# Layer 0 of a two-layer decoder trunk: where the low parts of the weights and the second group's scans stand in the order of work

## The chip, the core and the metric

The kernel runs on one core of one Trainium2 chip. The core has five engines that run side by side and meet at semaphores: TensorE (PE, matrix products into PSUM, with its weight loads shown as PEld), VectorE (DVE), ScalarE (ACT), GpSimd (POOL) and SyncE (SP, which here issues most of the DMAs). DVE and ACT work through their instructions in the order in which the program gives them. The metric is the device time of one execution in microseconds, and the median of several executions is compared.

## The reference

The program computes a decoder trunk of two layers for 256 tokens of width 2048, in float32. Layer 0 is RMSNorm, one input projection to 6144 columns, two mixers side by side, an output projection, a residual and a squared-ReLU MLP. Layer 1 has dilated attention in place of the mixers and the same MLP. Only the mixers of layer 0 matter here:

```python
proj = h @ w_in
x_lru, y_lru, q_h, f_h, v_h, g_h = jnp.split(proj, list(IN_SPLITS), axis=-1)
lru = rg_lru(causal_depthwise_conv(x_lru, conv_w, conv_b), w_a, b_a, w_i, b_i, lam)
lru = lru * jax.nn.gelu(y_lru.astype(F32), approximate=True)
hg = hgrn2(q_h, f_h, v_h, g_h, lower_bound, g_norm)
mixed = jnp.concatenate([lru, hg], axis=-1).astype(h.dtype)
return mixed @ w_out
```

`rg_lru` makes two gates with small block matrices, turns them into `a` and `u` (a tanh, an exp and a square root for each), and runs the recurrence h = a h + u over the 256 tokens; the GeLU of `y` multiplies the result. `hgrn2` is a gated linear attention with eight heads: it multiplies running products of its forget gate into queries and keys, forms scores, mixes the values, normalises each head and multiplies with SiLU of `g`.

## The kernel before

**Products in three parts.** Every float32 weight tile is split into a high part (a cast to fp32r on ACT, the tile `hi`) and the low rest (a subtraction on DVE, the tile `lo`, which reads the raw weights and `hi`). Activations are split in the same way. A product is then three matmuls: high by high, high by low, low by high. They sum into a PSUM tile `p`.

**Units.** The weights come in units of 128 x 2048 floats, 1 MB each. The input projection has twelve groups of 512 columns, four units each, in the order of the string `ORDER`: `v0 x0 x1 q0 G0 f0 q1 f1 G1 v1 g0 y0 g1 y1` (`G0` and `G1` are the two units of gate weights). A unit of the projection is 24 matmuls with 512 columns. In the trace they can be counted; the groups begin at about 123.7 us (`q1`), 182 (`v1`), 209.5 (`g0`), 237.2 (`y0`), 262.9 (`g1`), 289.8 (`y1`) and 314 (the first pass of the output projection, `o0`); its second pass (`o1`) begins at about 338. When a unit begins, `unit` calls `fetch` for the unit two places later: its DMA, its cast on ACT and its low part on DVE. There are three buffers each for raw, high and low.

**Side work in lanes.** The mixers' own work is cut into steps, written as Python generators that stand in five lanes. Lanes `a` and `b` hold the hgrn chains, two heads each (`hgrn(0)` and `hgrn(1)`, then `hgrn(2)` and `hgrn(3)`, the second group). One step of a chain has a few small matmuls on PE, then several DVE instructions, then copies on ACT (`kc`) which the next step's matmuls read. Lane `c` holds the convolution, then the GeLU (`lru_gelu`, two steps for each half) and its products with the recurrence (`lru_out`). Lane `d` holds the normalisation and gating of the heads (`finish`). Lane `e` holds `lru_scan`, four steps for each half of the recurrence: two steps with tanh and exp, then two with the square root and the scans.

**The order by hand.** `TICKS` says which steps are issued where: for each group of columns eight entries, two for each unit, one after the unit's 12th matmul and one after its 24th. The letters of an entry name the lanes that move on one step. From the group `x0` on, `InOrder` chains all DVE instructions in program order, and all ACT instructions likewise; `mm` and `turn` chain the instructions of PE. So an instruction's place in the program is its place in its engine's queue. This ends with the last unit of `o0`; after it the order of DVE and ACT is left to the framework's scheduler.

**The low parts.** While entries of `TICKS` remain, `split` does not issue the low part at once; it puts it in the list `lows`, and `settle` issues what waits there. `settle` is called at the start of each unit and after each entry. So the low part of the unit two places on is issued in the middle of a unit, behind all steps of the entry there. The lines that matter are these:

```python
if at_ % 4 == 3 and ticks:
    tick(ticks.pop(0))
    settle()
```

In the profile, DVE and ACT instructions stand at line 68 (the wrapper that issues them), matmuls at 255 and transposes through PE at 258. So the instructions are told apart by their tiles: `lo<-raw,hi` is a low part, `hi<-raw` a high part, `xall`, `st` and `kc` belong to the hgrn chains, `xc` and `bufb` with 128x256 to the scans, `tk<-p` copies a finished group of columns out of PSUM, `hs`, `rs`, `hr`, `z` and `ho` belong to `finish`, and `tk<-tk` to the GeLU.

Of the kernel before, what the change touches and what calls it, by code (L numbers as in the profile page):

```python
# [41 lines left out]
def trunk_kernel(ctx, tc, head, x, xtok, xback, cols, tab, masks, pos, fin, w_in, w_gate, w_out, w_qkv, w_o, w1, w2, out):  # L42
# [195 lines left out]
    def settle():  # L238
        with stream():
            while lows:  # L240
                lows.pop(0)()

    def unit(src, i):
        settle()
        u = at[1]
        assert units[u][0] is src and units[u][1] in (None, i), (u, i)
        at[1] += 1
        if u + 2 >= at[0]:
            fetch()
        return made.pop(u)  # L250
# [3 lines left out]
    def mm(*args, **kw):  # L254
        chain[:] = [after(T.matmul(*args, **kw), chain)]  # L255
# [12 lines left out]
    def turn_some(age=2):  # L268
        for t in turns:
            t[0] += 1  # L270
        for _ in range(2):
            if turns and turns[0][0] >= age:
                turns.pop(0)[1]()
# [88 lines left out]
    def tokens(src, i0, mov, kgs=(0, 1, 2, 3), by_k=False, behind=(), then=()):  # L362
        ks = PAIRED if src is w_o else range(KB)
        ps = [pmm.tile([P, 512], F32, name="p") for _ in range(2)]
        for g in kgs:
            w = unit(src, i0 + g)
            order = [(j, i) for i in range(4) for j in range(2)] if by_k else \
                [(j, i) for j in range(2) for i in range(4)]
            for at_, (j, i) in enumerate(order):
                k = ks[4 * g + i]  # L370
                h, l = w.part(i * 512, 512)
                xh = mov[:, k, j * P:j * P + P]
                xl = mov[:, k, S + j * P:S + j * P + P]
                first, last = g == kgs[0] and i == 0, g == kgs[-1] and i == 3
                if g == kgs[-1] and (i, j) == (1, 0):
                    chain.extend(behind)
                mm(ps[j], xh, h, start=first, stop=False)
                mm(ps[j], xh, l, start=False, stop=False)
                mm(ps[j], xl, h, start=False, stop=last)
                if at_ % 4 == 3 and ticks:  # L380
                    tick(ticks.pop(0))
                    settle()
            turn_some(1)
            for f in steps.pop(0) if steps else ():
                f()
            for m in then[kgs.index(g)] if then else ():
                mixed_forms(m)
        return ps

    def tick(which):  # L390
        for name in which.strip("."):
            with urgent():
                while lanes[name] and next(lanes[name][0], True):
                    lanes[name].pop(0)

    def tokens_group(step, rt=None, by_k=False, behind=()):
        ticks[:] = TICKS.get(step, "").split()
        ps = tokens(w_in, 4 * PLACE[step], bufa, by_k=by_k)
        v = vgs.tile([P, 2, 512], F32, name="tk", bufs=7)
        with urgent():  # L400
            for j in range(2):
                after(A.activation(v[:, j], ps[j], AF.Copy, scale=1.0 if rt is None else rt[:, j:j + 1]), behind)
        return v
# [224 lines left out]
    def lru_in(n, half):  # L628
        b0 = 4 * n + 2 * half
        p = turned("po", [done[f"x{n}"]] * 2, (2 * half, 2 * half + 1), back=True)  # L630
        for i in range(2):
            b = b0 + i
            A.activation(xc[:, b], p[:, i], AF.Identity, bias=col("conv_b", b), scale=col("conv_w", 24 + b))
            for t in range(3):
                V.scalar_tensor_tensor(xc[:, b, 3 - t:], p[:, i, :S - 3 + t], col("conv_w", 8 * t + b),
                                       xc[:, b, 3 - t:], op0=OP.mult, op1=OP.add)
            yield
        split_to(bufb[:, b0:b0 + 2], xc[:, b0:b0 + 2])
        yield
# [14 lines left out]
    def lru_scan(gp):  # L654
        gr, gi = rooms[gp][:, :4], rooms[gp][:, 4:]
        for half in range(2):
            for m in range(2 * half, 2 * half + 2):
                b = 4 * gp + m
                V.tensor_tensor(xc[:, b], xc[:, b], gi[:, m], OP.mult)
                lut(gi[:, m], gr[:, m], AF.Tanh, scale=sp4[:, b:b + 1])  # L660
                lut(gr[:, m], gr[:, m], AF.Exp, scale=sp8[:, b:b + 1])
                V.tensor_scalar(gi[:, m], gi[:, m], -1.0, 1e-30, op0=OP.mult, op1=OP.max)
            yield
        for half in range(2):
            for m in range(2 * half, 2 * half + 2):
                b = 4 * gp + m
                lut(gi[:, m], gi[:, m], AF.Sqrt)
                V.scalar_tensor_tensor(gi[:, m], gr[:, m], 1.0, gi[:, m], op0=OP.add, op1=OP.mult)
                V.tensor_tensor(xc[:, b], xc[:, b], gi[:, m], OP.mult)
                V.tensor_tensor_scan(xc[:, b], gr[:, m], xc[:, b], 0.0, op0=OP.mult, op1=OP.add)  # L670
            yield

    def lru_gelu(n):
        y = done[f"y{n}"]
        q = outs[f"y{n}"] = vgs.tile([P, 2, 512], F32, name="tk", bufs=7)
        for j in range(2):
            A.activation(q[:, j], y[:, j], AF.Square, scale=math.sqrt(0.044715))
            V.scalar_tensor_tensor(q[:, j], q[:, j], 1.0, y[:, j], op0=OP.add, op1=OP.mult)
            lut(q[:, j], q[:, j], AF.Sigmoid, scale=2.0 * math.sqrt(2.0 / math.pi))
            V.tensor_tensor(y[:, j], y[:, j], q[:, j], OP.mult)  # L680
            yield

    def lru_out(n, half):
        b0 = 4 * n + 2 * half
        p = turned("pt" if half else "pd", [done[f"y{n}"]] * 2, (2 * half, 2 * half + 1), back=True)
        z = outs[f"y{n}"][:, half].rearrange("p (i s) -> p i s", i=2)
        V.tensor_tensor(z, p, xc[:, b0:b0 + 2], OP.mult)
        split_to(bufb[:, b0:b0 + 2], z)
        yield

    def reload():
        for j in range(2):
# [3 lines left out]
                 c=[lru_in(0, 0), lru_in(0, 1), lru_in(1, 0), lru_in(1, 1),  # L696
                    lru_gelu(0), lru_out(0, 0), lru_out(0, 1), lru_gelu(1), lru_out(1, 0), lru_out(1, 1)],
                 e=[lru_scan(0), lru_scan(1)],
# [17 lines left out]
    def close_mixers():  # L716
# [4 lines left out]
        pair, formh = open_pairs(0)  # L721

    tick("c")
    ticks[:] = TICKS["o0"].split()
    steps[:] = [[], [], [close_mixers], [lambda: setattr(InOrder, "on", False)]]
# [42 lines left out]
    def mixed_forms(m):  # L768
        z = pair.tile([P, 2, 2, P], F32, name="y1", bufs=2)
        b = bufb[:, 2 * m:2 * m + 2].bitcast(F32)  # L770
        V.tensor_tensor(z.rearrange("p i j c -> p i (j c)"), b[..., :S], b[..., S:], OP.add)
        a11, a21, a12, a22 = (z[:, i, j] for i in range(2) for j in range(2))
        combos(a22, a11, a21, a12, a11, a21, a12, a22)
        part_forms(formh, m, 1, slice(0, 4), z.rearrange("p i j (one c) -> p one (i j) c", one=1))

    def out_project(src, gname, kgs, behind=()):
        nrm = Norm()
        whole = any(src is w for w in (w_out, w_o, ))
        for n in range(2 if whole else 4):
            then = () if not whole else ((((), (), (0, 1), (2,)), ((), (3,), (), ())) if src is w_out else  # L780
                                         (((), (), (), (0, 1)), ((), (2,), (3,), ())))[n]
            add_res(tokens(src, 4 * n, bufb, kgs, src is w_o and not n, () if n else behind, then), n, nrm)
            to_features(n, gname, formx if n < 2 else None)
        if whole:
            second(0, 2, nrm, 1.0, -1.0, lambda n: to_features(n, gname, None), None, src)
        return nrm
# [408 lines left out]
}  # L1195
PLACE = {step: n for n, step in enumerate(step for step in ORDER.split() if step[0] != "G")}
WARM = 12
# [102 lines left out]
```

## Time and profile before

| what | value |
|---|---|
| median of three runs | 2123.5 us (2123.3 to 2123.9) |
| profiled execution, its own time | 2124.2 us |
| its span, first to last instruction | 2122.4 us |
| granted TensorE clock, mean | 0.999 |
| PE busy | 2108.1 us, 99% of the span |
| DVE busy | 1782.4 us, 84% |
| ACT busy | 1316.9 us, 62% |
| share of PE in the chain that ended last | 94% |

The engine that is busy 99% of the span sets the time: what an edit on DVE or ACT is worth is read from the moments in which PE stands still. "Busy" counts a matmul from its start to its modelled end, and consecutive matmuls overlap, so a pause of PE is measured best between starts: matmuls with 512 columns start 0.23 us apart in this stage when nothing is late. A row of the timeline gives start, duration, engine, line, operation, output and inputs, shapes, a count where equal instructions follow one another, and in brackets the idle time of the engine before it with what ended that time.

### The profile page before, as it was taken

The numbers are of one execution on the slowest core, as the hardware profiler recorded it, in microseconds if no ns is written. First come the engines' busy times: TensorE is split into PE (matmuls) and PEld (weight loads), VectorE is DVE, ScalarE is ACT, GpSimd is POOL, SyncE is SP. The second block draws the span as 40 slices with busy tenths as digits, with TensorE's granted clock in tenths as the row PEclk, the third lists the DMA queues.
The fourth block names the chain that finished last, engine by engine and source line by source line (L and its number), as shares of the span: only waits on it lengthen the run. The fifth ranks groups of instructions, "written<-read, shape, count | busy, mean of one in ns | idle before, by whom it ended". The sixth has DMA issues, their size and how long they took to land.

```text
span 2122.4 us, 24764 instructions
## 1 busy us (share of the span) xinstructions
PE 2108.1 (99%) x9748; PEld 1754.6 (83%) x9748; DVE 1782.4 (84%) x1723; ACT 1316.9 (62%) x1353; POOL 72.3 (3%) x89
## 2 busy tenths in 40 slices
PE   9999999999999999999999999999999999999998
PEld 8888887888888888888888888888888888888886
DVE  6676768988888888888998888798988987988887
ACT  7666556675566566566665666566755655755764
POOL 0000000000000000000000000000000000000000
PEclk9999999999999999999999999999999999999999
DMA  8543456887788878777787667577787878788884
GB/s 345 179 159 141 178 197 214 246 261 241 249 258 256 253 234 269 254 239 243 255 257 245 214 210 242 178 233 237 242 253 263 243 240 281 238 247 249 267 261 154
DMA packets 70165, 500.15 MB, mean 236 GB/s; under 512 B 7840, under 2 KB 8096, under 8 KB 10272
## 3 DMA queue, kind: packets, MB, share of 16 engines
q1 hardware_dynamic: 57888, 413.03, 51.1%
q0 software_dynamic: 11872, 84.94, 21.5%
q8 instruction: 76, 1.25, 0.2%
q10 hardware_dynamic: 288, 0.61, 0.1%
q14 instruction: 41, 0.34, 0.0%
HBM read 496.44 MB, written 2.10 MB: 235 GB/s over the span
## 4 chain that ended last, share of the span: by engine, by line
PE 94%; DVE 3%; ACT 2%; issue 0%; ACTq 0%; DVEq 0%
PE p L255 59%; PE pd L255 15%; PE po L255 14%; PE pt L255 3%; PE pl L258 2%; PE pl L255 1%; DVE lo L68 1%; ACT hi L68 1%; ACT bufb L68 1%; DVE xc L68 0%; ACT ho L68 0%; PE po L315 0%; DVE bufb L68 0%; ACT L68 0%; ACT tk L68 0%
## 5 line engine op out<-in xcount | busy, mean ns | idle before, releaser
L68 ACT CAST hi<-raw 128x2048 fp32r<-128x2048 f32 (+1 forms) x364 | 659.4, 1817 | 463.0 <-PE p L255 270.8
L68 DVE TENSOR_TENSOR lo<-raw,hi 128x2048 fp32r<-128x2048 f32 (+1 forms) x364 | 788.3, 2170 | 173.2 <-ACT hi L68 172.4
L255 PE MATMUL p<-hi,bufa 128*128 128x512 f32 x2000 | 643.5, 392 | 0.0
L255 PEld LDWEIGHTS p<-hi,bufa 128*128 128x128 f32 x2000 | 375.7, 188 | 77.0
L255 PE MATMUL p<-hi,bufb 128*128 128x512 f32 x1264 | 405.1, 391 | 0.0
L255 PE MATMUL p<-lo,bufa 128*128 128x512 f32 x1000 | 389.7, 390 | 1.4 <-DVE lo L68 1.4
L68 DVE TENSOR_TENSOR lo<-s,hi 128x2048 fp32r<-128x2048 f32 x120 | 274.1, 2285 | 11.2 <-ACT hi L68 9.2
L255 PEld LDWEIGHTS p<-hi,bufb 128*128 128x128 f32 x1264 | 237.3, 188 | 49.2 <-ACT tk L68 0.2
L68 ACT CAST hi<-s 128x2048 fp32r<-128x2048 f32 x120 | 229.5, 1913 | 50.8 <-PE po L255 22.6
L255 PE MATMUL p<-lo,bufb 128*128 128x512 f32 x632 | 246.1, 389 | 1.1 <-DVE lo L68 1.1
L255 PEld LDWEIGHTS p<-lo,bufa 128*128 128x128 f32 x1000 | 188.0, 188 | 40.1 <-DVE lo L68 2.6
L255 PEld LDWEIGHTS p<-lo,bufb 128*128 128x128 f32 x632 | 118.7, 188 | 25.7 <-DVE lo L68 1.4
L255 PE MATMUL pd<-hi,bufa 128*128 128x512 f32 x352 | 116.8, 393 | 0.0
L255 PE MATMUL p<-hi,formx 128*128 128x512 f32 x352 | 116.3, 391 | 0.0
L68 DVE TENSOR_TENSOR lo<-t,hi 128x2048 fp32r<-128x2048 f32 x40 | 91.5, 2288 | 15.9 <-ACT hi L68 15.8
L255 PE MATMUL po<-hi,bufb 128*128 128x512 f32 (+1 forms) x320 | 102.4, 386 | 0.0
L255 PE MATMUL p<-hi,formh 128*128 128x512 f32 x288 | 94.5, 389 | 0.0
L68 DVE TENSOR_TENSOR s<-s,raw 128x2048 f32<-128x2048 f32 x40 | 91.3, 2282 | 2.2 <-DMA raw<-in_w_qkv 2.2
L68 DVE TENSOR_TENSOR s<-raw,t 128x2048 f32<-128x2048 f32 x40 | 91.3, 2283 | 0.5 <-DMA raw<-in_w_o 0.4
L68 ACT ACTIVATE y<-y 128x512 f32<-128x512 f32 x112 | 68.8, 629 | 28.0 <-DVE y L68 27.2
L255 PE MATMUL po<-hi,bufa 128*128 128x512 f32 x256 | 84.9, 393 | 0.0
L68 ACT CAST hi<-t 128x2048 fp32r<-128x2048 f32 x40 | 76.5, 1914 | 12.3 <-PE po L255 6.3
(298 smaller groups left out, 2784.4 us busy)
## 6 DMA issues: line engine op xcount, KB each, us to landing
raw<-in_w SPq DMA_DIRECT2D x224, 1024.0 KB, 6.4
raw<-in_w_in SPq DMA_DIRECT2D x45, 1024.0 KB, 4.8
raw<-in_w_qkv SPq DMA_DIRECT2D x42, 1024.0 KB, 7.0
t<-in_w SPq DMA_DIRECT2D x32, 1024.0 KB, 6.6
t<-in_w POOLq DMA_DIRECT2D x32, 1024.0 KB, 8.6
s<-in_w POOLq DMA_DIRECT2D x32, 1024.0 KB, 8.9
raw<-in_w_out SPq DMA_DIRECT2D x15, 1024.0 KB, 4.9
raw<-in_w_o SPq DMA_DIRECT2D x15, 1024.0 KB, 4.9
```

What stands on the lines that cost most here:

```text
L68: i = call(*args, **kw)
L255: chain[:] = [after(T.matmul(*args, **kw), chain)]
L258: chain[:] = [after(T.transpose(out_, in_, ident), chain)]
```

## The change

Three things change in the order written by hand; no instruction is added or removed.

First, where the low parts are issued. `settle` moves into `tick`. Ahead of a step of lane `c`, `d` or `e` the low part that waits is issued first; behind steps of `a` and `b` it is issued as before. Second, the four scan steps of the second group (`lru_scan(1)`) leave the entries of the group `v1`, where they stood at the first, second, fourth and fifth entry, and go to `g0`, one after the end of each unit. Third, in `o0` the two last `lru_out` steps move from the third and fourth entry to the fourth and fifth, half a unit later each.

```diff
                 mm(ps[j], xl, h, start=False, stop=last)
                 if at_ % 4 == 3 and ticks:
                     tick(ticks.pop(0))
-                    settle()
...
     def tick(which):
         for name in which.strip("."):
+            if name not in "ab":
+                settle()
             with urgent():
                 while lanes[name] and next(lanes[name][0], True):
                     lanes[name].pop(0)
+        settle()
...
-    "v1": "abe e ab e abe . ab .",
-    "g0": "ab . ab . ab . ab .",
+    "v1": "ab . ab . ab . ab .",
+    "g0": "ab e ab e ab e ab e",
     "y0": "ab d ab d ab . ab d",
     "g1": "ab d abc . abd c . d",
     "y1": "d c dd c . d . .",
-    "o0": "c . c c . . . .",
+    "o0": "c . . c c . . .",
```

## The prediction, made before the result was known

> **What bounds the kernel now.** I read the page first, then PE's waits over the whole span, then PE's timeline at each wait, then DVE's and ACT's there.
>
> ```profile
> PE 2108.1 (99%) x9748; PEld 1754.6 (83%) x9748; DVE 1782.4 (84%) x1723; ACT 1316.9 (62%) x1353; POOL 72.3 (3%) x89
> ```
>
> ```profile
> PE p L255 <- DVE lo L68: 2.5, 4, 1.1
> PE pd L258 <- DVE tk L68: 1.1, 1, 1.1
> ...
> PE pd L255 <- ACT st L68: 0.2, 1, 0.2
> ```
>
> PE sets the time, and apart from the first microsecond (the row left out) it waits only six times, all six between 124 and 346 us. Nothing that the change does to DVE or ACT is worth more than these waits, unless it makes new ones. Their true size is in the distance between starts:
>
> ```profile
> 123.48 0.39 PE L255 MATMUL p<-lo,bufa 128*128 128x512 f32 x1
> 123.70 0.61 PE L255 MATMUL p<-hi,bufa 128*128 128x512 f32 x2
> 124.48 0.50 PE L255 MATMUL p<-lo,bufa 128*128 128x512 f32 x1 [0.16 <-DVE lo L68]
> 124.83 0.64 PE L255 MATMUL p<-hi,bufa 128*128 128x512 f32 x2
> ...
> 209.32 0.61 PE L255 MATMUL p<-hi,bufa 128*128 128x512 f32 x2
> 210.98 0.50 PE L255 MATMUL p<-lo,bufa 128*128 128x512 f32 x1 [1.04 <-DVE lo L68]
> ...
> 240.01 1.05 PE L255 MATMUL pl<-xall,kc 128*128 128x128 f32 x8
> ...
> 246.35 1.05 PE L255 MATMUL pl<-xall,kc 128*128 128x128 f32 x8
> ...
> 266.66 0.48 PE L255 MATMUL p<-hi,bufa 128*128 128x512 f32 x1
> ...
> 308.69 0.50 PE L255 MATMUL p<-lo,bufa 128*128 128x512 f32 x1 [0.22 <-DVE lo L68]
> ...
> 323.69 0.55 PE L258 MATMUL pd<-tab__186,tk 128*128 128x128 f32 x3 [1.14 <-DVE tk L68]
> ...
> 345.59 0.50 PE L255 MATMUL p<-lo,bufb 128*128 128x512 f32 x1 [1.12 <-DVE lo L68]
> ```
>
> Matmuls start 0.23 apart (123.48 to 123.70), so the one at 124.48 is due at 123.70 + 0.46 = 124.16 and 0.32 late; that of `g0` is due at 209.78 and 1.20 late. Each is the bracket plus 0.16, since the bracket doesn't count the drain of the pipeline. By that rule `y1`'s wait at 308.69 is 0.38, the transposes' at 323.69 is 1.30, the one at 345.59 is 1.28. The `st` wait I take as its 0.2. After a wait for a low part the next start is 0.34 away, not 0.23 (124.48 to 124.83): 0.11 more for each.
>
> Within reach of the change are 0.32 + 0.20 + 1.20 + 0.38 + 1.30 = 3.40, and 3 x 0.11: 3.73 us. The wait at 345.59 (1.28 + 0.11 = 1.39) lies behind the order by hand.
>
> **Low parts ahead of c, d and e.** Rows of DVE:
>
> ```profile
> 119.17 0.40 DVE L68 SCALAR_TENSOR_TENSOR bufb<-bufb 128x256 f32<-128x256 f32 x1
> ...
> 122.17 2.27 DVE L68 TENSOR_TENSOR lo<-raw,hi 128x2048 fp32r<-128x2048 f32 x1
> ...
> 193.09 0.42 DVE L68 TENSOR_TENSOR xc<-xc,bufb 128x256 f32<-128x256 f32 x1
> ...
> 195.29 0.29 DVE L68 TENSOR_SCALAR bufb<-bufb 128x256 f32<-128x256 f32 x1 [0.58 <-ACT bufb L68]
> ...
> 205.63 0.43 DVE L68 SCALAR_TENSOR_TENSOR bufb<-bufb 128x256 f32<-128x256 f32 x1 [2.63 <-ACT bufb L68]
> ...
> 221.13 0.69 DVE L68 TENSOR_TENSOR xall<-xall 128x512 f32<-128x512 f32 x1 [4.23 <-ACT hi L68]
> ...
> 227.93 0.69 DVE L68 TENSOR_TENSOR xall<-xall 128x512 f32<-128x512 f32 x1 [2.12 <-issue]
> ...
> 234.32 0.69 DVE L68 TENSOR_TENSOR xall<-xall 128x512 f32<-128x512 f32 x1 [1.12 <-issue]
> ...
> 240.71 0.69 DVE L68 TENSOR_TENSOR xall<-xall 128x512 f32<-128x512 f32 x1 [1.36 <-ACT hi L68]
> ...
> 247.48 0.69 DVE L68 TENSOR_TENSOR xall<-xall 128x512 f32<-128x512 f32 x1
> ...
> 253.85 0.68 DVE L68 TENSOR_TENSOR xall<-xall 128x512 f32<-128x512 f32 x1
> ...
> 259.75 0.69 DVE L68 TENSOR_TENSOR xall<-xall 128x512 f32<-128x512 f32 x1 [1.45 <-issue]
> ...
> 264.11 0.47 DVE L68 SCALAR_TENSOR_TENSOR bufb<-po,c__91,bufb 128x256 fp32r<-128x256 f32 x1
> ...
> 285.35 2.28 DVE L68 TENSOR_TENSOR lo<-raw,hi 128x2048 fp32r<-128x2048 f32 x1
> 287.54 0.68 DVE L68 SCALAR_TENSOR_TENSOR tk<-tk 128x512 f32<-128x512 f32 x1
> ...
> 306.36 2.28 DVE L68 TENSOR_TENSOR lo<-raw,hi 128x2048 fp32r<-128x2048 f32 x1
> ...
> 321.56 0.69 DVE L68 SCALAR_TENSOR_TENSOR tk<-tk 128x512 f32<-128x512 f32 x1 [1.72 <-ACT tk L68]
> ...
> 323.56 2.35 DVE L68 TENSOR_TENSOR lo<-raw,hi 128x1024 fp32r<-128x1024 f32 x2
> ```
>
> `q1`: the low part at 122.17 stands behind a square-root step that starts at 119.17. Ahead of it, it ends at about 121.5, needed at 124.16: the wait goes. The step ends 3.00 later, at 124.4, where it delays the chains by 0.1 at most.
>
> `y1`: the low part at 306.36 goes ahead of the two steps of lane `d` in its entry and is in time. The steps behind it lose up to 2.28, and PE transposes their result right before 308.69. But the same rule moves the low part at 285.35 ahead of a step of lane `d` too, and the GeLU behind it (287.54), with the casts behind that, comes some 2 us earlier. One pays the other; I take 0 for a new wait, and 1.1 as its upper end (half of 2.28).
>
> `o0`: before, the GeLU's last product released the transposes at 323.69. Now two low parts (2.35 at 323.56) go ahead of the GeLU's second half, but DVE idles 1.72 there, so the product is 0.63 late: 324.3. The transposes go half a unit later, 12 x 0.227 = 2.7 us: from 322.4 to 325.1. The wait goes, with 0.8 to spare. The last `lru_out` is half a unit nearer to the unit that reads it; 0, upper end 0.25.
>
> **Scan steps out of v1.** There the low part for `g0` stood behind the last scans, which waited 2.63 for ACT (205.63). Without them it follows its cast, and the waits of 1.20 and 0.2 go.
>
> **Scan steps in g0.** A tanh step costs DVE 195.29 + 0.29 - 193.09 = 2.49, a square-root step 122.17 - 119.17 = 3.00. In `v1` the chains had nearly no DVE work; in `g0` each unit has 4.7 to 5.3 us of it in 6.4. ACT's rows:
>
> ```profile
> 187.91 0.51 ACT L68 ACTIVATE bufb<-bufb,sp 128x256 f32<-128x256 f32 x1 [3.16 <-DVE xc L68]
> 188.44 1.28 ACT L68 ACT_TABLE_LOAD   x1
> 189.74 1.45 ACT L68 ACTIVATE bufb<-bufb,sp 128x256 f32<-128x256 f32 x3
> ...
> 217.30 1.12 ACT L68 ACTIVATE xall<-xall,lb,omlb 128x256 f32<-128x256 f32 x2
> ...
> 242.56 0.50 ACT L68 COPY kc<-xall 128x128 f32<-128x128 f32 x2 [0.64 <-DVE xall L68]
> ...
> 264.99 1.26 ACT L68 ACTIVATE tk<-p,nr 128x512 f32<-128x512 f32 x2
> ```
>
> I keep count of how late DVE begins a chain step, against the moment when PE's small matmuls are ready (0.70 behind their row: 240.01, 240.71). Own work between two starts is the distance less the idle time in the second row's bracket.
>
> - First tanh step: ACT is free at 217.30 + 1.12 = 218.42; the step takes 3.06 from there, as in `v1`: tanh at 187.91, table load, exp at 189.74, second tanh 0.41 later with 0.51, scaling on DVE with 0.29, end at 190.97. So DVE is free at 221.48, 0.35 late at 221.13.
> - At 227.93: 0.35 + (6.80 - 2.12) + 2.49 - 6.80 = 0.72.
> - At 234.32: 0.72 + (6.39 - 1.12) + 3.00 - 6.39 = 2.60.
> - At 240.71: 2.60 + (6.39 - 1.36) + 3.00 - 6.39 = 4.24.
> - Next is ready at 240.71 + 6.34 (PE, 240.01 to 246.35) = 247.05: 4.24 + 6.77 - 6.34 = 4.67.
> - At 253.40: 4.67 + 6.37 - 6.35 = 4.69. At 259.75: 4.69 + (5.90 - 1.45) - 6.35 = 2.79. Then it falls.
>
> PE needs the second chain's `kc` 0.44 into its next small matmuls, 6.35 - 0.70 + 0.44 = 6.09 after DVE's due start; DVE and ACT take 243.06 - 240.71 = 2.35 for it. So 3.74 of lateness are hidden. New waits in `y0`: 4.24 - 3.74 = 0.50, then 4.67 - 0.50 - 3.74 = 0.43, then 0.02: 0.95 together. A low part has more room: it is used one and a half units (9.5) behind its entry and ready 0.70 + 2.3 + 2.3 behind it, which leaves 4.2.
>
> Behind DVE stands ACT, behind ACT the copy of PSUM that frees PE's next buffer (`tk<-p`). In `y0` two square roots go ahead of it: 0.1. In `g1`, DVE is 2.79 - 0.95 - 0.1 = 1.74 late at 264.11; ACT's next cast waits for that, then the first copy ends at 264.99 + 0.69 + 1.74 = 267.42, and PE wants the buffer at 266.66: 0.76. New waits: 0.95 + 0.1 + 0.76 = 1.81. Lower end 0, if DVE's steps overlap better than my sum; upper end 1.81 + 1.1 + 0.25 = 3.16.
>
> No step moved here issues a DMA; the weights' DMAs stay at the starts of units, so the queues of SP and POOL are as before.
>
> **Sum.** -3.73 + 1.81 = -1.92 against the profiled execution's 2124.2. The median is 2123.5; from it, 2121.6 us. Ends: -3.73 (2119.8) and -0.57 (2122.9).
>
> **A rule against it.** The row at 188.44 is a table switch: 1.28, and the next activation at 189.74, 0.02 behind it; the change keeps three switches, but in `g0` and `y0` they meet a late DVE. The Trainium skill, "ScalarE: Activation LUTs", section "What ACT_TABLE_LOAD costs", gives about 1283 ns for the load and about 1380 ns more for a drain. The row bears out the first and shows no drain. By the page two switches in `g0` would add an estimated 2.8 us of lateness and waits, and the sum would be 2124.4.
>
> **Rivals.**
>
> - *All cover holds, and the wait at 345.59 goes too* (the framework orders DVE anew behind `o0`): -3.73 - 1.39 = 2118.4. For it: DVE still idles 1.1 to 4.2 in each unit of `g0`. Against: the sum above. Chance 0.15. Only one of the two: 2119.8 to 2120.2, 0.22.
> - *Slower: the square-root steps wait for ACT in `g0` as at 205.63.* ACT's roots stand behind `kc` copies that wait for a late DVE, and a table switch. Two waits of 2.63 are 5.26 more lateness with no cover left: 2126.9. It decides for slower once the waits added pass 3.73, that is 1.92 beyond my sum. For it: the same steps did so in `v1`. Against: the low part now stands between and gives ACT 2.28. Chance 0.12, half of it beyond 2127.7; the page's drain is 0.03 more, at 2124.4.
> - *The move does nothing where PE waits* (the wait only passes to the next late step of the same queue): 2123.5, 0.10.
>
> **Chances.** Forecast (2120.4 to 2122.9) 0.38. The bound for a difference is 0.2%, 4.25 us, about what a measurement of this kernel tells from no change. Faster than 2119.25: the first rival, 0.15. Slower than 2127.75: 0.06. Within: 0.79. The range is 2118.3 to 2124.4, ends of the first rival and of the page's case; the forecast's own is 2119.8 to 2122.9.
>
> **What would show it.** In the profile after: no wait for `lo` at the first unit of `q1`, of `g0`, or the last of `y1`, and none at `pd<-tab,tk` in `o0`; scans (`xc`) in `g0` between the low parts; DVE busy without idle from `g0` to the middle of `y0`; PE waits of 0.1 to 0.8 on `kc` or `p` in `y0` and at `g1`'s first unit. Wrong would be waits over 1 us in `y0`, or a new one in `o0` or `o1` over 1.4.

## The result, and the profile after

The median fell from 2123.73 us (2123.3 to 2125.1) to 2119.00 us (2118.6 to 2120.6), a ratio of 0.9978 with a 95% interval of 0.9970 to 0.9986. The profiled execution took 2118.8 us against 2124.2, its span 2117.0 against 2122.4.

The page of the changed kernel, the line of the engines, and then its waits of PE (us in total, times, longest):

```profile
PE 2107.0 (100%) x9748; PEld 1755.6 (83%) x9748; DVE 1783.4 (84%) x1723; ACT 1316.2 (62%) x1353; POOL 72.4 (3%) x89
```

```profile
PE po L315 <- DVE e L68: 1.1, 1, 1.1
PE p L255 <- DVE lo L68: 0.4, 1, 0.4
PE p L255 <- ACT tk L68: 0.4, 1, 0.4
```

No engine is busy for more than 1.1 us more or less than before. Of the six waits that the prediction listed, five are gone (the first units of `q1` and `g0`, the `st` wait, the last unit of `y1`, the transposes in `o0`) and the sixth, in `o1`, has shrunk. A new one is listed at `g1`'s first unit.

Medians of this kernel move by 1 us for reasons that will be shown, so waits are compared over one stretch that all kernels share: from the first transposes of `q1` to a matmul that opens a unit behind `o1`. PE's timeline, the kernel before and then the changed one:

```profile
120.32 0.60 PE L258 MATMUL pd<-tab__186,tk 128*128 128x128 f32 x4
...
402.62 0.39 PE L255 MATMUL po<-hi,bufb 128*128 128x512 f32 x1
```

```profile
120.57 0.60 PE L258 MATMUL pd<-tab__186,tk 128*128 128x128 f32 x4
...
237.94 1.05 PE L255 MATMUL pl<-xall,kc 128*128 128x128 f32 x8
...
244.29 1.24 PE L255 MATMUL pl<-xall,kc 128*128 128x128 f32 x8
...
250.86 1.35 PE L255 MATMUL pl<-xall,kc 128*128 128x128 f32 x8
...
257.55 1.09 PE L255 MATMUL pl<-xall,kc 128*128 128x128 f32 x8
...
264.43 1.05 PE L255 MATMUL pl<-xall,kc 128*128 128x128 f32 x8
265.86 0.50 PE L255 MATMUL p<-hi,bufa 128*128 128x512 f32 x1 [0.37 <-ACT tk L68]
...
342.20 0.50 PE L255 MATMUL p<-lo,bufb 128*128 128x512 f32 x1 [0.40 <-DVE lo L68]
...
399.10 0.39 PE L255 MATMUL po<-hi,bufb 128*128 128x512 f32 x1
```

The stretch is 402.62 - 120.32 = 282.30 us before and 399.10 - 120.57 = 278.53 after: 3.77 less. It repeats: 282.19 in another execution of the kernel before, 278.55 in another of the changed one. Inside it the rows show the price paid. The groups of small matmuls of `y0` come 6.35 apart where nothing waits (237.94 to 244.29), then 6.57 and 6.69. At 265.86 PE waits again.

The other part of the gain stands at the very end. Traffic of a window of 7 us about the end in 40 slices, and the last output transfer (KB, median us from issue to landing), before and then after:

```profile
GB/s 0 0 0 0 0 0 351 421 468 421 374 445 421 375 398 351 421 515 374 398 164 0 23 23 23 23 23 23 0 0 0 0 0 0 0 0 0 0 0 0
...
out<-xall ACTq DMA_DIRECT2D x1, 512.0 KB, 4.5
```

```profile
GB/s 47 0 0 0 0 0 0 0 0 0 0 0 0 328 398 398 445 468 374 445 422 398 421 374 445 468 398 211 0 0 0 0 0 0 0 0 0 0 0 0
...
out<-xall ACTq DMA_DIRECT2D x1, 512.0 KB, 3.2
```

Before, the transfer ends with 1 us at 23 GB/s, about a sixteenth of the rate ahead of it; after, it doesn't. 3.8 us of waits and 1.3 us here are 5.1; the medians differ by 4.7.

### The profile page after: what moved, and what is told of

It is laid out like the page before. It is cut to its first block, busy times and chain, and to the rows that moved or that the text cites. A ratio compares the mean times of both kernels' runs of the same rounds, so it can differ in the third digit from the quotient of the medians.

```text
span 2117.0 us, 24774 instructions
## 1 busy us (share of the span) xinstructions
PE 2107.0 (100%) x9748; PEld 1755.6 (83%) x9748; DVE 1783.4 (84%) x1723; ACT 1316.2 (62%) x1353; POOL 72.4 (3%) x89
## 4 chain that ended last, share of the span: by engine, by line
PE 98%; DVE 1%; ACT 0%; issue 0%; DVEq 0%; ACTq 0%
PE p L255 62%; PE pd L255 15%; PE po L255 14%; PE pt L255 3%; PE pl L258 2%; PE pl L255 1%; DVE lo L68 0%; PE po L315 0%; DVE xall L68 0%; PE po L258 0%; DVE y L68 0%; ACT hi L68 0%; PE pd L258 0%; PE pt L258 0%; ACT xall L68 0%
```

## The experiments

The kernels' stretches (each from the same two rows of its own trace) and medians in one table. "Last transfer" is the time of the last output transfer, as in the fences above.

| kernel | stretch, us | against before | median, us | ratio (95%) | last transfer |
|---|---|---|---|---|---|
| before, again | 282.19 | -0.11 | 2124.05 | 1.0002 (0.9993 to 1.0011) | 4.2 |
| the change, again | 278.55 | -3.75 | 2119.01 | 0.9979 (0.9970 to 0.9988) | 3.2 |
| low parts alone | 277.39 | -4.91 | 2118.22 | 0.9974 (0.9964 to 0.9984) | 3.2 |
| low parts alone, again | 277.43 | -4.87 | 2119.27 | 0.9979 (0.9970 to 0.9988) | 3.2 |
| scans alone | 281.67 | -0.63 | 2123.39 | 0.9999 (0.9991 to 1.0008) | 4.1 |
| products alone | 285.05 | +2.75 | 2125.41 | 1.0008 (0.9999 to 1.0017) | 4.5 |
| low parts and products | 277.77 | -4.53 | 2119.27 | 0.9978 (0.9969 to 0.9987) | 3.2 |
| low parts and scans | 278.19 | -4.11 | 2119.95 | 0.9978 (0.9969 to 0.9987) | 3.2 |
| low parts, two scans moved | 276.90 | -5.40 | 2117.65 | 0.9972 (0.9962 to 0.9982) | 3.2 |
| the same, again | 276.90 | -5.40 | 2117.89 | 0.9974 (0.9964 to 0.9984) | 3.2 |
| products alone, order ended earlier | 281.03 | -1.27 | 2122.41 | 0.9993 (0.9984 to 1.0001) | 3.2 |
| before, DVE's program 8 longer | 282.25 | -0.05 | 2122.87 | 0.9993 (0.9984 to 1.0002) | 3.3 |

**The kernel before, unchanged.**

> The kernel before once more, unchanged. It shows what two executions of one program differ by in the start, the long part behind the mixers and the last DMA. Theory: the 5.4 us between the two profiled spans are 3.75 us of PE's waits and some 1.6 us of such differences; so this run lies within 0.05% of 2123.7, and its time from the last ScalarE instruction to the end of the span may differ from 5.7 us by a microsecond. Rival: the span's tail and the long part are the same in every execution, and the rest of the gain is the change's own.

Stretch and waits repeat within 0.1 us, and the last transfer ends slowly again (4.2).

**The low parts alone.** The order by hand stays as it was; only `settle` moves:

```diff
                 if at_ % 4 == 3 and ticks:
                     tick(ticks.pop(0))
-                    settle()
...
         for name in which.strip("."):
+            if name not in "ab":
+                settle()
...
+        settle()
```

> Only the new place of settle: low parts ahead of steps of lanes c, d and e; scans stay in v1, o0 as before. Theory (the low parts are what PE waited for, wherever the scans stand): the waits at q1, at g0's first unit and at y1's last unit go, 0.32 + 1.20 + 0.38 + 0.33; the wait of 0.2 for st stays, and that at the transposes in o0 shrinks but stays, since the GeLU comes earlier by 1 to 2 us. 2120.5 to 2121.3, with no waits in y0. Rival, as my prediction had it (the wait at g0 goes because the scans leave v1): g0's wait stays near 1.2, 2121.7 to 2122.2.

It gains 4.91 in the stretch, 1.1 more than the whole change. The median of 2118.22 lies 2.3 below what was expected, because the wait in `o1` and the slow end of the last transfer went too. PE's waits, rows of PE's timeline, and rows of DVE's, with the low part for `g0` in the kernel before ahead of them:

```profile
PE pd L255 <- ACT st L68: 0.2, 1, 0.2
```

```profile
320.52 0.92 PE L258 MATMUL pd<-tab__186,tk 128*128 128x128 f32 x4
321.19 0.48 PE L255 MATMUL p<-hi,bufb 128*128 128x512 f32 x1
```

```profile
208.66 2.27 DVE L68 TENSOR_TENSOR lo<-raw,hi 128x2048 fp32r<-128x2048 f32 x1
```

```profile
203.12 2.27 DVE L68 TENSOR_TENSOR lo<-raw,hi 128x2048 fp32r<-128x2048 f32 x1
...
318.76 0.69 DVE L68 SCALAR_TENSOR_TENSOR tk<-tk 128x512 f32<-128x512 f32 x1
```

The low part for `g0` starts at 203.12 in place of 208.66, ahead of the last scans that still stand in `v1`, and ends 4.6 us before PE wants it (209.97). So it wasn't the scans' place that cost 1.20 at `g0`, but the low part's place behind them. In `o0` the GeLU's second half starts at 318.76 against 321.56 before, 2.80 earlier, while PE is about 1.8 earlier there. Of the transposes' wait 0.31 is left (320.52 to 321.19 is 0.67, and 0.36 where nothing waits), with the products where they had stood. And the wait in `o1` is gone altogether.

**The scans alone.**

```diff
-    "v1": "abe e ab e abe . ab .",
-    "g0": "ab . ab . ab . ab .",
+    "v1": "ab . ab . ab . ab .",
+    "g0": "ab e ab e ab e ab e",
```

> Only the scan steps of the second group from v1 to g0; low parts behind all steps, o0 as before. Theory: g0's wait (1.2 + 0.11) and the wait for st (0.2 to 0.4) go, but y0 and g1's first unit get 1.3 us of new waits for kc and p, as in the changed kernel; the others stay: 2123.0 to 2124.2, no gain. Rival: the scans cost nothing in g0, the waits in y0 come from the low parts ahead of lane d: 2121.9 to 2122.3.

```profile
PE p L255 <- DVE lo L68: 1.5, 3, 1.1
PE pd L258 <- DVE tk L68: 1.2, 1, 1.2
...
PE p L255 <- ACT tk L68: 0.4, 1, 0.4
```

The waits at `g0` and on `st` go (1.8 in the stretch), and 1.3 comes back in `y0` and at `g1`'s first unit, the last row. Either edit removes the wait at `g0`; this one pays for it.

**The products alone.**

```diff
-    "o0": "c . c c . . . .",
+    "o0": "c . . c c . . .",
```

> Only the two last lru_out steps half a unit later. Theory: the wait at the first transposes in o0 (1.3 to 1.5) goes: 2122.1 to 2122.5, unless the last lru_out comes too late for the unit that reads it, which would give a part of it back. Rival: without the low parts ahead the product of the GeLU and the low parts behind it push the second lru_out into the unit that reads it, a new wait of about 1: 2123.3.

The transposes don't wait, as predicted (-1.5 by 330 us), but the stretch is 2.75 longer. PE's timeline behind the last transposes of `o0`; ACT's rows, first of the kernel before and then of this one; PE in windows (busy us and count of PE, PEld, DVE, ACT, POOL, then the granted clock):

```profile
342.47 0.60 PE L258 MATMUL pl<-tab__186,xall 128*128 128x128 f32 x4
344.93 0.50 PE L255 MATMUL p<-hi,bufb 128*128 128x512 f32 x1 [1.86 <-ACT hi L68]
346.19 0.79 PE L255 MATMUL p<-lo,bufb 128*128 128x512 f32 x1 [0.76 <-DVE lo L68]
346.78 1.05 PE L255 MATMUL p<-hi,bufb 128*128 128x512 f32 x2
...
348.06 1.05 PE L255 MATMUL p<-hi,bufb 128*128 128x512 f32 x2
```

```profile
342.86 3.89 ACT L68 CAST hi<-raw 128x1024 fp32r<-128x1024 f32 x4
```

```profile
331.51 0.61 ACT L68 CAST bufb<-tk 128x512 fp32r<-128x512 f32 x1
...
342.56 0.62 ACT L68 CAST formh<-y 128x512 fp32r<-128x512 f32 x1 [3.38 <-DVE y L68]
343.11 0.84 ACT L68 ACTIVATE y<-pl,c__91 128x256 f32<-128x256 f32 x2
343.83 4.83 ACT L68 CAST hi<-raw 128x1024 fp32r<-128x1024 f32 x5
```

```profile
345.00:347.00 2.00, 1.24 (x3) 0.83 (x4) 2.00 (x3) 2.00 (x3) 0.00 (x0) 0.61 0.00 0
347.00:349.00 2.00, 2.00 (x6) 1.52 (x6) 2.00 (x4) 2.00 (x3) 0.00 (x0) 0.50 0.41 66
...
351.00:353.00 2.00, 2.00 (x7) 1.55 (x6) 2.00 (x4) 0.17 (x1) 0.00 (x0) 0.68 1.05 438
```

ACT's casts for `o1` stand behind a cast (`formh`) that waits 3.38 for DVE, and behind two activations that came after them before. They start at 343.83, 0.97 later than before (342.86), while PE, having waited less in `o0`, is there 1.2 earlier. PE waits 1.86 for the first of them. Then the granted clock falls to 0.50, while PE stands still again, for 0.76: three matmuls take 1.28 (346.78 to 348.06) in place of 0.68. The 15 matmuls from 346.19 to 352.54 cost 6.35 in place of 15 x 0.227 = 3.4, so the clock alone costs 2.9.

**Products alone, the order by hand ended one unit earlier.**

```diff
-    "o0": "c . c c . . . .",
+    "o0": "c . . c c . . .",
...
-    steps[:] = [[], [], [close_mixers], [lambda: setattr(InOrder, "on", False)]]
+    steps[:] = [[], [], [close_mixers, lambda: setattr(InOrder, "on", False)], []]
```

> The products' move alone, and the order by hand ends one unit earlier, so that the high parts of the units behind it may be issued ahead of the mixed forms' casts. Theory: in the run of the move alone PE waited 1.9 for a high part that stood in ACT's hand-made order behind a late cast, and the clock fell to a half because PE had stood still; so here no wait on a high part, granted clock 1.0 from 345 to 353 us, and the wait for a low part in o1 about as before the change (1.4) or less: 2122.3 (2121.2 to 2122.6) against 2125.4. Rival for the clock: it falls at this place whatever PE waits for, or by chance: 0.5 again, and 2124.5 or more. Rival for the wait: the late forms alone make it, wherever the order ends: 2124.5 to 2125.5.

```profile
347.00:349.00 2.00, 2.00 (x11) 1.64 (x10) 2.00 (x3) 1.44 (x4) 0.00 (x0) 1.00 0.79 242
```

```profile
334.84 0.50 PE L255 MATMUL p<-hi,bufb 128*128 128x512 f32 x1 [1.29 <-ACT bufb L68]
```

```profile
332.28 2.00 ACT L68 CAST hi<-raw 128x1024 fp32r<-128x1024 f32 x2 [0.23 <-PE p L255]
334.18 0.61 ACT L68 CAST bufb<-tk 128x512 fp32r<-128x512 f32 x1
```

No wait on a high part, and the clock stays at 1.00; the 2.75 loss becomes a gain of 1.27. PE now waits 1.29 for the last product itself (`bufb`, at 334.84). That isn't the half unit by which the product moved: the run before has the same move, its cast of the product stands at 331.51, and PE doesn't wait there. Here ACT does weight casts first (332.28), and the cast of the product at 334.18 behind them. So the lost time of the run before was the late casts and the half clock behind them. The wait and the fall of the clock went together, and this run doesn't part the one from the other.

**Two of three parts.** The change with the scans left in `v1`, and the change with the products left where they stood. Both have the new place of `settle`, and the edits show what they have beside it:

```diff
-    "o0": "c . c c . . . .",
+    "o0": "c . . c c . . .",
```

> Low parts and GeLU products as in the change, scans left in v1. Theory: the new waits of the change (1.34 us in y0 and at the first unit of g1) come from the scans in g0 alone, and with the low parts first the products' move is worth nothing; so no wait in y0 and g1, only the 0.2 on st, and 2118.2 (2117.6 to 2118.8), as with the low parts alone. Rival: the products' move costs something by itself, through the late last product: a wait of 0.57 or more at the last unit of o1, as in the change, and 2118.8 to 2119.3. Second rival: as in the run of the products' move alone, a high part comes late in o1 and the clock is halved: 2121 or more.

```diff
-    "v1": "abe e ab e abe . ab .",
-    "g0": "ab . ab . ab . ab .",
+    "v1": "ab . ab . ab . ab .",
+    "g0": "ab e ab e ab e ab e",
```

> Low parts and scans as in the change, GeLU products where they stood before. Theory: the waits in y0 and at the first unit of g1 are there as in the change, 1.2 to 1.4 us in all, the transposes in o0 and o1's last unit wait for nothing, as with the low parts alone: 2118.2 + 1.3 - 0.2 (the st wait, gone with the scans in g0) = 2119.3. Rival: the wait of 0.57 in o1 belongs to the lateness that the scans push through, and stays: 2119.9. Second rival: the late DVE makes the transposes wait again unless the products move: over 2120.

PE's waits that tell the two apart, first of low parts and products, then of low parts and scans:

```profile
PE p L255 <- DVE lo L68: 0.6, 2, 0.4
PE pd L255 <- ACT st L68: 0.2, 1, 0.2
```

```profile
PE p L255 <- ACT tk L68: 0.4, 1, 0.4
```

That the products' move would be worth nothing with the low parts first was wrong: 0.4 of the first row stands in `o1`, as the rival had it. The stretch makes a square, all with the low parts first:

| | products where they stood | products half a unit later |
|---|---|---|
| scans in `v1` | -4.91 | -4.53 |
| scans in `g0` | -4.11 | -3.77 |

The scans' move costs 0.80 and 0.76, the products' 0.38 and 0.34: each by itself, and they add. Read by place, the scans give 0.5 at the `st` wait and take 1.3 in `y0` and `g1`; the products give 0.3 at the transposes and take 0.7 in `o1`, where of these four kernels PE waits for a low part exactly in the two with late products. The medians (2118.2 to 2120.0) don't order these kernels, because of the next point.

**The change again, beside them.**

> The changed kernel again, beside the three others. Theory: 2119.0, with the same waits (1.1 and 0.4 on the chains' results, 0.4 on a low part in o1), 0.8 above the runs with the scans left in v1, of which 1.34 are the waits in y0 and g1, 0.57 that in o1, less the 0.2 on st; their sum, 1.7, would put it 1.7 above and not 0.8. Rival: the waits differ from one execution to the next, and the sum of the mean execution is 0.8.

The same waits and the same stretch: they don't differ from one execution to the next. The sum of 1.7 in the expectation left out the 0.3 that the products' move gives back at the transposes, and had the `st` wait 0.3 and the one in `o1` 0.1 too low: 1.7 - 0.3 - 0.3 + 0.1 = 1.2, and the stretches differ by 278.53 - 277.39 = 1.14.

**Low parts first, two scan steps in each group.** The edit against the low parts alone:

```diff
-    "v1": "abe e ab e abe . ab .",
-    "g0": "ab . ab . ab . ab .",
+    "v1": "ab e ab e ab . ab .",
+    "g0": "ab e ab e ab . ab .",
```

> Low parts first, and the scan steps on every other entry of v1 and g0, so that two steps stand in v1 and two in g0. Theory: the scans make waits only where DVE falls behind by more than its cover of 3.74 us, and two steps leave it under that; so no wait in y0 or g1 and none on st: 2118.2 - 0.2 = 2118.0 (2117.5 to 2118.6). Rival: any scan step in g0 makes a wait in y0 or g1: 2118.6 to 2119.3.

No wait from 20 to 400 us, 276.90 for the stretch, the shortest of all, though ACT has one more table load (12 for 11). Its profiled execution shows why single times spread. DVE's row, and PE's, in layer 1:

```profile
1301.47 2.29 DVE L68 TENSOR_TENSOR s<-s,raw 128x2048 f32<-128x2048 f32 x1 [2.41 <-DMA raw<-in_w_qkv]
```

```profile
1307.28 0.50 PE L255 MATMUL p<-lo,bufa 128*128 128x512 f32 x1 [1.33 <-DVE lo L68]
```

A weight transfer lands up to 2 us later in some executions (DVE waits 0.3 to 2.4 for it), and PE then loses up to 1.6: 1.6 in this execution, 0.2 in the next one of the same kernel.

**That kernel and the low parts alone on one chip.**

> Low parts first, two scan steps in v1 and two in g0, the products where they stood; again, beside the low parts alone. Theory: no wait from 20 to 400 us, and 2117.7, 0.2 to 0.5 under the low parts alone. Rival: the two are the same within 0.2, and the difference of the two earlier calls was the chip's.

> The low parts alone again, on the same chip as the run with two scan steps moved. Theory: 2118.2, with the wait of 0.2 on st as the only one from 20 to 400 us. Rival: 2117.7, as the run beside it.

2117.89 and 2119.27, stretches 276.90 and 277.43. The stretch gives 0.5 of the 1.4 between the medians, the `st` wait. Another 0.3 stands behind the start of the last matmul (8.41 us to the end of the span, against 8.68); the rest isn't explained by these two places. Two scan steps in each group is the best version found: it has the shortest stretch, and in both runs a median below those of the changed kernel, 2117.65 against 2119.01 on one chip. The intervals of these ratios overlap, so the order of the medians alone isn't certain.

**The kernel before with eight idle writes on DVE.** They stand beside the gate unit `G1`, where DVE waits anyway:

```diff
             lru_gates(int(step[1]))
+            for k in range(8 * int(step[1])):
+                V.memset(pads[:, k:k + 1], 0.0)
```

> The kernel before with eight idle writes of one element per lane added on DVE beside the gate unit G1, so that DVE's program is as many instructions longer as with the low parts moved; nothing else. Theory: about 1.0 us of the change's gain isn't a wait of PE. In the profiles of before, and of the runs of the scans alone and the products alone, a fetch of instructions lands amid the last output transfer, one DMA engine finishes last alone at 23 GB/s, and the transfer takes 4.1 to 4.5 us; with the low parts moved it takes 3.2. DVE's eight more instructions move that fetch: the transfer 3.2, no stretch at 23 GB/s, PE's waits as before, and 2122.6 against 2123.6. Rival: the length of the last transfer goes with something else that the change does, or it is another engine's fetch: 4.1 to 4.5 again, and 2123.6 (2123.3 to 2124.0).

```profile
GB/s 0 0 47 0 0 0 0 0 0 0 0 0 47 468 398 374 421 398 421 421 375 398 374 445 398 445 398 211 0 0 0 0 0 0 0 0 0 0 0 0
...
out<-xall ACTq DMA_DIRECT2D x1, 512.0 KB, 3.3
```

The stretch is that of before (282.25), the tail of 23 GB/s is gone, and the transfer takes 3.3. The median is 2122.87 against 2124.44 of the kernel before on that chip, but the interval of the ratio reaches past 1, so the medians alone don't show the gain. The traces do: from the start of the last matmul to the end of the span the four executions with the slow end take 9.27 to 9.65 us, this one 8.48, and the nine others 8.40 to 8.68. DVE's program is longer in the kernels with the low parts first, too: they hold 7 or 8 more semaphore instructions on DVE (523 or 524 for 516), though the change adds no work. So about 1 us of the change's gain isn't due to a wait of PE, and DVE's longer program is enough to bring it.

In the traces a fetch of instructions (8 KB, the slices with 47) falls amid the last transfer in the four executions with the slow end, and ahead of it or behind it in the others. That it is the fetch that holds one DMA engine up fits all these traces; it wasn't isolated from other effects of a longer program, and the fetch itself takes 0.3 to 0.5 us, less than the 1 us lost.

## Why the prediction was right, and where it wasn't

The time of 2119.0 lies inside the range of 2118.3 to 2124.4, and the sign was right, but the number was 2.6 too high. It lies below the forecast's own 2119.8 to 2122.9, and just past the bound of 2119.25, beyond which the prediction saw a chance of 0.15; a difference within its bound, 0.79, was what it held likely. The wider range held it by luck in part: its lower end came from a rival whose mechanism didn't come true, and about 1 us of the gain stands where the prediction had no term. By place (starts of the same matmul in the two traces, us):

| place | predicted | the change | low parts alone |
|---|---|---|---|
| `q1`, low part | -0.43 | -0.49 | -0.49 |
| the `st` wait in `v1` | -0.20 | -0.44 | +0.06 |
| `g0`, low part | -1.31 | -1.37 | -1.38 |
| new waits in `y0`, `g1` | +1.81 | +1.33 | 0 |
| `y1`, low part | -0.49 | -0.51 | -0.51 |
| `o0`, transposes | -1.30 | -1.44 | -1.11 |
| `o1`, low part | 0 | -0.79 | -1.47 |
| rest of the stretch | 0 | -0.06 | -0.03 |
| last transfer | 0 | -1.3 | -1.3 |

*The waits taken away.* Right in place and size, with the drain of 0.16 and the slower restart of 0.11 that the bracket leaves out: `q1`, `g0`, `y1` within 0.1. The `st` wait was worth 0.44, twice its bracket.

*"Scan steps out of v1": the step that failed.* It gave `g0`'s wait to the scans' departure. The low parts alone remove it, with the scans in `v1`. The rule of the same change, a low part ahead of `e`, had already taken it away, so the scans' move bought the `st` wait only. Either part removes the wait at `g0` without the other, as the run of the scans alone shows.

*"Scan steps in g0".* The count of lateness held. Rows of DVE in the changed kernel, the low part for `q1` and then the chain steps, and of ACT at the first table switch:

```profile
120.06 2.27 DVE L68 TENSOR_TENSOR lo<-raw,hi 128x2048 fp32r<-128x2048 f32 x1
...
231.43 0.42 DVE L68 SCALAR_TENSOR_TENSOR bufb<-bufb 128x256 f32<-128x256 f32 x1
...
242.38 0.67 DVE L68 TENSOR_TENSOR xall<-xall 128x512 f32<-128x512 f32 x1
...
249.13 0.69 DVE L68 TENSOR_TENSOR xall<-xall 128x512 f32<-128x512 f32 x1
...
255.52 0.68 DVE L68 TENSOR_TENSOR xall<-xall 128x512 f32<-128x512 f32 x1
```

```profile
216.77 1.28 ACT L68 ACT_TABLE_LOAD   x1
218.07 1.45 ACT L68 ACTIVATE bufb<-bufb,sp 128x256 f32<-128x256 f32 x3
```

Against PE's small matmuls plus 0.70, DVE is 242.38 - 238.64 = 3.74 late, then 249.13 - 244.99 = 4.14, then 255.52 - 251.56 = 3.96. The prediction had 4.24 for the first and, less the waits made by then, 4.17 and 3.76. The waits came out 0.22, 0.34 and 0.07 in `y0`, for 0.50, 0.43 and 0.12, and 0.70 at `g1`, for 0.76: 1.33 for 1.81, near enough, too high at the first. The lateness that was hidden before a wait came out at 3.5 to 3.9 (3.74 - 0.22, 4.14 - 0.34, 3.96 - 0.07), where the prediction had 3.74. DVE was without idle time from 226 to 264 us, not from the start of `g0`: with the first tanh steps it still waits for ACT.

*The slower rival* fell: the square-root steps start without a wait (231.43 has no bracket). *The table switch* takes 1.28, and the next activation starts 0.02 behind it. The Trainium skill, "ScalarE: Activation LUTs", section "What ACT_TABLE_LOAD costs", has a drain of about 1380 ns more; this trace shows none, as before, and the rival drawn from it fell.

*"o0".* The wait went, but the working was wrong on both sides. It had the product 0.63 later than before, behind the low parts, so that only the half unit saved it; the low parts alone show it nearly in time at its old place (0.31 late). And the "last `lru_out` half a unit nearer, 0" costs 0.7 in `o1`, against an upper end of 0.25.

*"The wait at 345.59 lies behind the order by hand"*, taken as unchanged: wrong. It was 1.39 before, 0.7 with the products late, 0 with the low parts alone. So it hangs on how early DVE and ACT get through `o0`. The rival that had this wait go (2118.4, 0.15) came nearest in the number, but not in the mechanism: half of the wait went, and its other condition, that all cover holds, failed by 1.33 in `y0` and `g1`.

*Outside the sum.* 3.77 of waits are 1.85 more than forecast (0.79 in `o1`, 0.48 too much for the new waits, 0.24 at `st`, 0.14 at the transposes, the rest small). The other 0.8 to 1.3 is the last transfer, which no row of the prediction looked at.

## What to carry to other kernels

Ask of each of several edits what it does once the others are in: here one edit removed nearly all that the other two were for, and these then cost 0.8 and 0.4. On an engine with an order by hand, work that the bounding engine waits for goes ahead of work that has a unit to spare, and the steps of the side work are spread until no queue falls behind by more than its cover. Where the question is a few us, compare distances between the same two matmuls in two traces (they repeat within 0.1), not medians, and look at the last transfer too.

## What the runs showed of the hardware that wasn't expected

The granted clock fell to 0.50 in the run of the products alone after a single wait of 1.86 us. The window from 345 to 347 has a mean of 0.61 between 1.00 and 0.50, so the fall came 2 x 0.11 / 0.50 = 0.44 us into it, at 345.4, when the wait was over for half a microsecond and before the second one, of 0.76, had passed. The window from 351 to 353 (0.68) puts the return at 352.3, 6.8 us later. The Trainium skill, "TensorE: Matmul & The Clock Gate", section "What's actually happening", names one idle window of about 3.4 us as what throttles, and a window that runs freely. Here the 3.4 us before the fall weren't idle throughout: PE stood still for 1.86 of them and worked for the other 1.5 (up to 343.07, and from 344.93). A wait of 1.29, in the run with the order ended earlier, left the clock at 1.00, and so did one of 1.12 at the same place in the kernel before. Where between 1.29 and 1.86 it turns, and whether the place in the window decides, no run here shows.

Eight DVE instructions that do nothing took the slow end off the last output transfer: 3.3 us in place of 4.1 to 4.5, and 0.8 to 1.2 us less from the last matmul to the end of the span.
